# Left factors of a Strassen output projection formed in two portions, and gate rows and background sums issued under conditions

## Chip, cores and metric

The program runs on one NeuronCore of a Trainium2 chip. The metric is device time in microseconds (us), shown as the median of several runs; beside it stands one execution recorded by the hardware profiler, whose rows are used below. Engines: PE is TensorE, DVE is VectorE, ACT is ScalarE, POOL is GpSimd, SP issues the DMAs.

## What is computed

One hybrid streaming-encoder block on x of 1024 frames by 2048 channels, in float32:

```
mod = silu(c) @ w_ada + b_ada          # shift, scale, gate: 2048 each
h = rms(x) * norm_g * (1 + scale) + shift
a_q, a_k, a_v, a_z, g_q, g_f, g_i, g_z = split(h @ w_in)     # 8 groups of 1024 columns, 8 heads of 128
att = chunk_attention(a_q, a_k, a_v) * silu(a_z)   # each 64-frame chunk sees itself and 8 chunks before
hg  = hgrn2(g_q, g_f, g_i) * silu(g_z)             # gated linear recurrence, chunkwise
out = x + gate * (concat(att, hg) @ w_out)
```

## The kernel before

**Precision.** Every large product is made of three float32r matmuls: an operand is split into `hi`, a float32r copy written by ACT, and `lo`, the rest, written by DVE as a subtraction; the product is hi·hi + hi·lo + lo·hi. A matmul of 128 by 512 columns is the unit of TensorE's work.

**Input projection.** It runs head by head. A head has four slices of 192 matmuls: two slices `all` (q, k, v, i; each half of the frames), one `qf` (g_q and g_f, transposed) and one `zz` (both gate paths, transposed). The order is set by the list `slices` and the loop at L1037; the last head goes `qf`, `all`, `all`, `zz`. A slice fills four PSUM banks (`pj`), and at its end ACT and DVE evacuate them. Weights come in tiles `wraw`, fetched four steps ahead by SP and split two steps ahead (`ahead`, L982).

**Work in the background.** Attention (`att_mix`, L533), recurrence (`hg_mix`, L670) and the preparation of the output projection's right factors (`gate_gen`, L818, and then `wout_gen`, L853) are Python generators. The schedule is written out by hand: `run_ready` (L487) is called after each unit of matmuls, and lets every generator whose due time `st.t` has passed, by a model of the engines' times (`Engine`, costs at L45 to L61), issue its next piece. So the order of instructions on each engine is fixed when the program is built. A piece issued early waits on its engine, and what is behind it in that engine's queue waits too. `V.free` and `PE.free` are the model's times at which DVE and PE are done with what was issued; `wait(us)` puts a generator's due time that far behind PE's.

**Gate rows and right factors.** `gate_gen` sums the 2048 gate values in rows while heads 0 to 2 run. `wout_gen` then does, for each half q of the output columns: fetch the row sums `gl` from DRAM, split them (`ghi`, `glo`), sum them over the partitions on PE by a product with ones into the PSUM tile `gb`, and copy that to `gateb`. `gb` has the one buffer of the PSUM tag `ma`, which attention's score tile `att` uses too. Then, for each j of 0 to 7, it fetches two row blocks of w_out (`wor`), waits 20 us, multiplies both by the gate (DVE, 128x1024 each), forms five sums of quarter blocks (DVE, 128x512) and stores seven factors to `wdr`.

**Output projection.** Its seven products follow Strassen's scheme, in the order of `CHAIN` (L1001): m = 2, 3, 4, 5, 1, 6, 7, for q = 0 and then q = 1. A product has eight steps j, a step four units of three matmuls. Right factors come from `wdr`; the left factors of a pair j of blocks of the mixed activations are, with a11, a12, a21, a22 its four quarters: m = 1: a11 + a22; 2: a21 + a22; 3: a11; 4: a22; 5: a11 + a12; 6: a21 - a11; 7: a12 - a22. `out_sums` (L637) forms all five sums on DVE at once. For j = 0 to 6 the blocks were stored to `odr` and `reload_o` (L988) fetches them while the last slice runs: it is called at the end of each step kk of that slice (L1086), and the right and left factors of the first two steps are split there as well (L1088). For j = 7, the last head, `finish` (L648) calls `out_sums` as soon as both parts exist, which is after the last slice (its gate path is the last thing projected). `right_split` and `left_split` (L1011, L1020) make `whi`, `wlo` and `ahl` two steps ahead of PE.

Of the kernel before, what the change touches and what calls it, by code (L numbers as in the profile page):

```python
# [21 lines left out]
NK = D // 128  # L22
# [81 lines left out]
def tile_hymba(ctx, tc, x, c, norm_g, w_ada, b_ada, w_in, q_norm_g, k_norm_g, rel_bias,  # L104
# [428 lines left out]
    def att_mix(h, st, direct):  # L533
# [39 lines left out]
        for i in range(NT):  # L573
# [4 lines left out]
            n = i - j0 + 1  # L578
            w = n * 128
            p = MA("att")  # L580
            qs = slice(i * 128, (i + 1) * 128)
            m = sm.tile([128, 4], F32, tag="mstat", name="mstat", bufs=3)
# [35 lines left out]
            for j in range(n):  # L618
                PE.matmul(o, st["v"][:, j0 + j, :], PT[:, j * 128:(j + 1) * 128], start=(j == 0),
                          stop=(j == n - 1))  # L620
            A.activation(oT[:, qs], o, AF.Copy)
            yield
        done.add(("att", h))
# [13 lines left out]
    def out_sums(j, a11, a12, a21, a22):  # L637

        y, z = (hp.tile([128, 1024], F32, tag="h", name=n) for n in ("oay", "oaz"))
        a7 = half_tile(j)  # L640
        V.tensor_add(y[:, 512:1024], a21, a22)
        V.tensor_add(y[:, 0:512], a11, a22)
        V.tensor_add(z[:, 0:512], a11, a12)
        V.tensor_sub(z[:, 512:1024], a21, a11)
        V.tensor_sub(a7, a12, a22)
        OA[j] = {1: y[:, 0:512], 2: y[:, 512:1024], 3: a11, 4: a22, 5: z[:, 0:512], 6: z[:, 512:1024], 7: a7}

# [205 lines left out]
    def wout_gen():  # L853

        for q in range(2):
            a, hi, lo = T4("gl"), T4("ghi", dt=F32R), T4("glo", dt=F32R)
            DMA.dma_start(a, gdr[q])
            A.activation(hi, a, AF.Copy)
            V.tensor_sub(lo, a, hi.bitcast(F32))
            yield  # L860
            p = MA("gb")
            for s in (slice(0, 512), slice(512, 1024)):
                PE.matmul(p[:, s], onesr.to_broadcast([128, 128]), hi[:, s], start=True, stop=False)
                PE.matmul(p[:, s], onesr.to_broadcast([128, 128]), lo[:, s], start=False, stop=True)
            gate = T4("gateb")
            A.activation(gate, p, AF.Copy)
            gate = gate.rearrange("p (a b) -> p a b", a=2)
            yield
            for j in range(NH):
# [4 lines left out]
                yield  # L874
                V.tensor_mul(r1, r1, gate)
                yield
                V.tensor_mul(r2, r2, gate)
                yield
                b11, b12, b21, b22 = r1[:, 0, :], r1[:, 1, :], r2[:, 0, :], r2[:, 1, :]
                for ma, mb, fa, fb in ((1, 3, (V.tensor_add, b11, b22), (V.tensor_sub, b12, b22)),  # L880
                                       (4, 6, (V.tensor_sub, b21, b11), (V.tensor_add, b11, b12))):
                    o = T4("wos", (128, 2, 512))
                    fa[0](o[:, 0, :], *fa[1:])
                    yield
                    fb[0](o[:, 1, :], *fb[1:])
                    wait(2.0)
                    yield
                    DMA.dma_start(wdr[q, ma - 1, j], o[:, 0, :])
                    DMA.dma_start(wdr[q, mb - 1, j], o[:, 1, :])
                    if ma == 1:  # L890
                        DMA.dma_start(wdr[q, 1, j], b11)
                        DMA.dma_start(wdr[q, 4, j], b22)
                V.tensor_add(b21, b21, b22)
                wait(2.0)
                yield
                DMA.dma_start(wdr[q, 6, j], b21)

    def wait(us):
# [89 lines left out]
    def reload_o(j):  # L988

        oa, ob = (odr[slot[order[i]]] for i in (2 * j, 2 * j + 1))  # L990
        x_ = hp.tile([128, 1024], F32, tag="h", name="oax")
        r = T4("orl")
        DMA.dma_start(x_[:, 0:512], oa[:, 0:512])
# [43 lines left out]
    for sl in slices:  # L1037
        kind, h, half = sl
        sa, sh = st_att[h], st_hg[h]
        ps = [pj.tile([128, 512], F32, tag="pj", name="pj") for _ in range(4)]  # L1040
        if kind == "all":
            for k in range(NK):
                n = first[sl] + k
                w = W.get(n)
                for u in range(4):
                    ahead(n, u)
                    wide_unit(ps[u], hhi[k], hlo[k], 4 * half + u, w, k)
                    if k == NK - 1:
                        evac_all(sa, sh, ps[u], 4 * half + u)
                    run_ready()  # L1050
# [4 lines left out]
        else:  # L1055
            if sl == slices[0]:
                rest = MH("rest", (128, 256))
            for kk in range(8):
                n = first[sl] + kk * (2 if sl == slices[0] else 1)
                w = W.get(n)  # L1060
                last = kk == 7
                for u in range(4):
                    ahead(n, u)
                    b, hf = u // 2, u % 2
                    for i in range(2):
# [10 lines left out]
                if sl == slices[0]:  # L1076
# [6 lines left out]
                    if last:  # L1083
                        evac_vi(sa, sh, rest, 7)
                        done.update((("v", 0), ("v", NH)))
                if sl == slices[-1] and kk >= 1:  # L1086
                    reload_o(kk - 1)
                if sl == slices[-1] and kk >= 6:  # L1088
                    right_dma(2 * kk - 10)
                    right_split(kk - 6)  # L1090
                    left_split(kk - 6)
            if sl == ("zz", 0, 0):
# [51 lines left out]
    banks = [[pj.tile([128, 512], F32, tag="pj", name="pjo") for _ in range(4)], None]  # L1144
    n = 0
    for q in range(2):
        C = {}
        for m, s_, fresh in CHAIN:
# [4 lines left out]
            for j in range(NH):  # L1153
                for u in range(4):
# [13 lines left out]
                    PE.matmul(b, hl[:, 1, ts], whi, start=False, stop=last, skip_group_check=True)  # L1168
                    run_ready()
                    if last:  # L1170
                        if m == 2:
# [63 lines left out]
```

## Time and profile before

| what | us |
|---|---|
| median of 3 runs (2048.43 to 2049.7) | 2049.66 |
| the profiled execution's own time | 2050.44 |
| its span, first to last instruction | 2048.6 |
| PE busy in the span | 2005.3 |
| DVE busy | 1182.3 |
| ACT busy | 713.8 |

The span is what the profile's rows count in, from 0 to 2048.6; the execution's own time is 1.84 us longer. Busy PE time is not the same as PE at its peak: a row's duration includes the depth of the array, so the pace of matmuls is read from the distance of their starts. All instructions of the engines carry L87, the helper that records them; they are told apart by their tiles (`pj` input projection, `pjo` and `po` output projection, `gb` gate broadcast, `lv` and `Amat` the recurrence's levels). The input projection lasts to 1729.76, the output projection from there to the end.

### The profile page before, as it was taken

The numbers are of one execution on the slowest core, as the hardware profiler recorded it, in microseconds if no ns is written. First come the engines' busy times: TensorE is split into PE (matmuls) and PEld (weight loads), VectorE is DVE, ScalarE is ACT, GpSimd is POOL, SyncE is SP. The second block draws the span as 40 slices with busy tenths as digits, with TensorE's granted clock in tenths as the row PEclk, the third lists the DMA queues.
The fourth block names the chain that finished last, engine by engine and source line by source line (L and its number), as shares of the span: only waits on it lengthen the run. The fifth ranks groups of instructions, "written<-read, shape, count | busy, mean of one in ns | idle before, by whom it ended". The sixth has DMA issues, their size and how long they took to land.

```text
span 2048.6 us, 30420 instructions
## 1 busy us (share of the span) xinstructions
PE 2005.3 (98%) x11329; PEld 1654.9 (81%) x11329; DVE 1182.3 (58%) x2038; ACT 713.8 (35%) x1659; POOL 97.6 (5%) x104
## 2 busy tenths in 40 slices
PE   5999999999999999999999999999999999999999
PEld 4678878888888788888788888888888787888887
DVE  6885654466446545674467456533454547548547
ACT  6454323322332233223322332233221343454453
POOL 1540000000000000000000000000000000000000
PEclk9999999999999999999999999999999999999999
DMA  9982134324432453446445634132112234337336
GB/s 340 341 240 75 52 93 132 95 86 134 131 98 83 126 158 125 149 140 196 125 133 166 190 122 137 54 111 68 42 48 76 83 98 144 93 98 247 109 97 227
DMA packets 308234, 269.50 MB, mean 132 GB/s; under 512 B 20515, under 2 KB 250995, under 8 KB 308085
## 3 DMA queue, kind: packets, MB, share of 16 engines
q1 hardware_dynamic: 307828, 267.49, 42.8%
q8 instruction: 89, 1.46, 0.3%
q14 instruction: 61, 0.49, 0.1%
q0 software_dynamic: 256, 0.06, 0.0%
HBM read 221.32 MB, written 46.15 MB: 131 GB/s over the span
## 4 chain that ended last, share of the span: by engine, by line
PE 93%; DVE 3%; DMA 2%; ACT 1%; issue 1%; POOL 0%; SPq 0%; ACTq 0%; DVEq 0%; POOLq 0%
PE pj L87 62%; PE pjo L87 8%; PE po L87 6%; PE att L87 6%; PE pjn L87 2%; PE pjC L87 2%; PE lv L87 2%; PE hgo L87 1%; PE pjB L87 1%; DMA x<-in_x_dram 1%; PE qkT L87 1%; PE hgU L87 1%; PE xTp L87 1%; PE hgoT L87 0%; DVE Amat L87 0%
## 5 line engine op out<-in xcount | busy, mean ns | idle before, releaser
L87 DVE TENSOR_TENSOR wlo<-wraw,whi 128x512 fp32r<-128x512 f32 x488 | 336.2, 690 | 483.0 <-ACT whi L87 478.1
L87 ACT ACTIVATE whi<-wraw 128x512 fp32r<-128x512 f32 x488 | 307.3, 630 | 733.1 <-PE pj L87 500.9
L87 PE MATMUL pj<-hh,whi 128*128 128x512 f32 x1024 | 411.8, 402 | 0.4 <-ACT v L87 0.4
L87 PE MATMUL pj<-hl,whi 128*128 128x512 f32 x1024 | 400.0, 391 | 0.0
L87 PE MATMUL pj<-hh,wlo 128*128 128x512 f32 x1024 | 399.6, 390 | 0.0
L87 PE MATMUL pj<-whi,hh 128*128 128x512 f32 x896 | 357.9, 399 | 0.9 <-DVE z L87 0.5
L87 PE MATMUL pj<-whi,hl 128*128 128x512 f32 x896 | 350.3, 391 | 0.0
L87 PE MATMUL pj<-wlo,hh 128*128 128x512 f32 x896 | 349.7, 390 | 0.0
L87 PEld LDWEIGHTS pj<-hl,whi 128*128 128x128 f32 x1024 | 192.2, 188 | 41.6
L87 PEld LDWEIGHTS pj<-hh,whi 128*128 128x128 f32 x1024 | 192.5, 188 | 36.8 <-ACT v L87 0.8
L87 PEld LDWEIGHTS pj<-hh,wlo 128*128 128x128 f32 x1024 | 192.8, 188 | 34.3
L87 PEld LDWEIGHTS pj<-whi,hl 128*128 128x128 f32 x896 | 168.5, 188 | 36.2
L87 PEld LDWEIGHTS pj<-whi,hh 128*128 128x128 f32 x896 | 168.8, 188 | 35.3 <-DVE z L87 1.8
L87 PEld LDWEIGHTS pj<-wlo,hh 128*128 128x128 f32 x896 | 168.9, 188 | 31.6
L87 PE MATMUL pjo<-whi,ahl 128*128 128x512 f32 x512 | 161.2, 394 | 3.8 <-DVE ahl L87 3.7
L87 PE MATMUL po<-whi,ahl 128*128 128x512 f32 x384 | 119.2, 389 | 0.0
L87 PEld LDWEIGHTS pjo<-whi,ahl 128*128 128x128 f32 x512 | 97.3, 190 | 25.0 <-DVE ahl L87 4.5
L87 PE MATMUL pjo<-wlo,ahl 128*128 128x512 f32 x256 | 100.7, 393 | 2.1 <-DVE wlo L87 2.1
L87 ACT ACTIVATE P<-att,mstat 128x640 f32<-128x640 f32 (+2 forms) x64 | 42.4, 662 | 165.6 <-DVE mstat L87 165.6
L87 PEld LDWEIGHTS po<-whi,ahl 128*128 128x128 f32 x384 | 72.1, 188 | 15.0
L87 PE MATMUL po<-wlo,ahl 128*128 128x512 f32 x192 | 74.7, 389 | 0.0
L87 PEld LDWEIGHTS att<-PT,v 128*128 128x128 f32 x480 | 63.1, 191 | 5.6
(240 smaller groups left out, 2300.9 us busy)
## 6 DMA issues: line engine op xcount, KB each, us to landing
wraw<-in_w_in_dram SPq DMA_DIRECT2D x240, 192.0 KB, 3.1
wraw<-in_w_in_dram SPq DMA_DIRECT2D x272, 128.0 KB, 2.8
wada<-in_w_ada_dram SPq DMA_DIRECT2D x64, 512.0 KB, 8.1
wraw<-wdr SPq DMA_DIRECT2D x112, 256.0 KB, 2.7
wadag<-in_w_ada_dram SPq DMA_DIRECT2D x64, 256.0 KB, 2.8
wor<-in_w_out_dram SPq DMA_DIRECT2D x32, 512.0 KB, 5.5
wdr<-wos SPq DMA_DIRECT2D x64, 256.0 KB, 2.1
wraw<-in_w_in_dram SPq DMA_DIRECT2D x240, 64.0 KB, 2.9
```

The source lines that it names most:

```text
L87: return f(*a, **kw)
```

## The change

Five edits. `att_mix` and `wout_gen` mark in `done` when the one `ma` buffer holds a score tile or the gate broadcast, and each waits, before it asks for the buffer, until the other's mark is gone. `wout_gen` waits 8 us between the fetch of the row sums and their split, and 5 us between the split and the matmuls. `wout_gen`'s two gate multiplications become four of half the size, and each of its DVE instructions is issued only if the model has DVE free for 0.3 us and no slice is at its edge (the mark `edge`: the last two steps of an `all` slice, the last of another). `out_sums` forms only the sum of m = 2; the other four sums of each j are formed by `more_sums`, partly in place of a12 and a21, one after the second and one after the fourth unit of each step of the products m = 3 and m = 4 of q = 0. In the last slice `reload_o` and the first splits move from the end of a step to after its first unit is prepared (u = 1; u = 0 in the last step); the second reloaded tile comes from the pool `hp` and not from `big`.

```diff
--- before.py
+++ after.py
@@ -577,7 +577,11 @@
             j0 = max(0, i - 4)
             n = i - j0 + 1
             w = n * 128
+            while "gb" in done:
+                wait(0.3)
+                yield
             p = MA("att")
+            done.add("ma")
             qs = slice(i * 128, (i + 1) * 128)
             m = sm.tile([128, 4], F32, tag="mstat", name="mstat", bufs=3)
             Pt = sm.tile([128, 640], F32, tag="P", name="P")
@@ -619,6 +623,7 @@
                 PE.matmul(o, st["v"][:, j0 + j, :], PT[:, j * 128:(j + 1) * 128], start=(j == 0),
                           stop=(j == n - 1))
             A.activation(oT[:, qs], o, AF.Copy)
+            done.discard("ma")
             yield
         done.add(("att", h))
         yield from need(("z", h))
@@ -636,14 +641,18 @@
 
     def out_sums(j, a11, a12, a21, a22):
 
-        y, z = (hp.tile([128, 1024], F32, tag="h", name=n) for n in ("oay", "oaz"))
+        y = hp.tile([128, 1024], F32, tag="h", name="oay")
         a7 = half_tile(j)
         V.tensor_add(y[:, 512:1024], a21, a22)
-        V.tensor_add(y[:, 0:512], a11, a22)
-        V.tensor_add(z[:, 0:512], a11, a12)
-        V.tensor_sub(z[:, 512:1024], a21, a11)
-        V.tensor_sub(a7, a12, a22)
-        OA[j] = {1: y[:, 0:512], 2: y[:, 512:1024], 3: a11, 4: a22, 5: z[:, 0:512], 6: z[:, 512:1024], 7: a7}
+        OA[j] = {1: y[:, 0:512], 2: y[:, 512:1024], 3: a11, 4: a22, 5: a12, 6: a21, 7: a7}
+
+    def more_sums(j):
+
+        o = OA[j]
+        for f, m, a, b in ((V.tensor_add, 1, 3, 4), (V.tensor_sub, 7, 5, 4), (V.tensor_add, 5, 3, 5),
+                           (V.tensor_sub, 6, 6, 3)):
+            f(o[m], o[a], o[b])
+            yield
 
     def finish(kt, oT, direct):
 
@@ -855,15 +864,25 @@
         for q in range(2):
             a, hi, lo = T4("gl"), T4("ghi", dt=F32R), T4("glo", dt=F32R)
             DMA.dma_start(a, gdr[q])
+            wait(8.0)
+            yield
             A.activation(hi, a, AF.Copy)
             V.tensor_sub(lo, a, hi.bitcast(F32))
-            yield
+            wait(5.0)
+            yield
+            while "ma" in done:
+                wait(0.3)
+                yield
             p = MA("gb")
             for s in (slice(0, 512), slice(512, 1024)):
                 PE.matmul(p[:, s], onesr.to_broadcast([128, 128]), hi[:, s], start=True, stop=False)
                 PE.matmul(p[:, s], onesr.to_broadcast([128, 128]), lo[:, s], start=False, stop=True)
             gate = T4("gateb")
             A.activation(gate, p, AF.Copy)
+            done.add("gb")
+            wait(1.5)
+            yield
+            done.discard("gb")
             gate = gate.rearrange("p (a b) -> p a b", a=2)
             yield
             for j in range(NH):
@@ -872,16 +891,18 @@
                     DMA.dma_start(r.rearrange("p a b -> p (a b)"), wout_v[:, order[e], q * 1024:(q + 1) * 1024])
                 wait(OUTPACE)
                 yield
-                V.tensor_mul(r1, r1, gate)
-                yield
-                V.tensor_mul(r2, r2, gate)
-                yield
+                for r in (r1, r2):
+                    for i in range(2):
+                        yield from idle()
+                        V.tensor_mul(r[:, i, :], r[:, i, :], gate[:, i, :])
+                        yield
                 b11, b12, b21, b22 = r1[:, 0, :], r1[:, 1, :], r2[:, 0, :], r2[:, 1, :]
                 for ma, mb, fa, fb in ((1, 3, (V.tensor_add, b11, b22), (V.tensor_sub, b12, b22)),
                                        (4, 6, (V.tensor_sub, b21, b11), (V.tensor_add, b11, b12))):
                     o = T4("wos", (128, 2, 512))
+                    yield from idle()
                     fa[0](o[:, 0, :], *fa[1:])
-                    yield
+                    yield from idle()
                     fb[0](o[:, 1, :], *fb[1:])
                     wait(2.0)
                     yield
@@ -890,10 +911,17 @@
                     if ma == 1:
                         DMA.dma_start(wdr[q, 1, j], b11)
                         DMA.dma_start(wdr[q, 4, j], b22)
+                yield from idle()
                 V.tensor_add(b21, b21, b22)
                 wait(2.0)
                 yield
                 DMA.dma_start(wdr[q, 6, j], b21)
+
+    def idle():
+
+        while V.free > PE.free - 0.3 or "edge" in done:
+            wait(0.3)
+            yield
 
     def wait(us):
         Engine.cur.t = max(Engine.cur.t, PE.free) + us
@@ -988,8 +1016,7 @@
     def reload_o(j):
 
         oa, ob = (odr[slot[order[i]]] for i in (2 * j, 2 * j + 1))
-        x_ = hp.tile([128, 1024], F32, tag="h", name="oax")
-        r = T4("orl")
+        x_, r = (hp.tile([128, 1024], F32, tag="h", name=n) for n in ("oax", "oar"))
         DMA.dma_start(x_[:, 0:512], oa[:, 0:512])
         DMA.dma_start(x_[:, 512:1024], ob[:, 512:1024])
         DMA.dma_start(r[:, 0:512], ob[:, 0:512])
@@ -1036,12 +1063,15 @@
 
     for sl in slices:
         kind, h, half = sl
+        done.discard("edge")
         sa, sh = st_att[h], st_hg[h]
         ps = [pj.tile([128, 512], F32, tag="pj", name="pj") for _ in range(4)]
         if kind == "all":
             for k in range(NK):
                 n = first[sl] + k
                 w = W.get(n)
+                if k >= NK - 2:
+                    done.add("edge")
                 for u in range(4):
                     ahead(n, u)
                     wide_unit(ps[u], hhi[k], hlo[k], 4 * half + u, w, k)
@@ -1059,8 +1089,16 @@
                 n = first[sl] + kk * (2 if sl == slices[0] else 1)
                 w = W.get(n)
                 last = kk == 7
+                if last:
+                    done.add("edge")
                 for u in range(4):
                     ahead(n, u)
+                    if sl == slices[-1] and u == (kk < 7) and kk >= 1:
+                        reload_o(kk - 1)
+                        if kk >= 6:
+                            right_dma(2 * kk - 10)
+                            right_split(kk - 6)
+                            left_split(kk - 6)
                     b, hf = u // 2, u % 2
                     for i in range(2):
                         tr_unit(ps[u], 2 * kk + i, hf, w, i, slice(b * 128, (b + 1) * 128))
@@ -1083,12 +1121,6 @@
                     if last:
                         evac_vi(sa, sh, rest, 7)
                         done.update((("v", 0), ("v", NH)))
-                if sl == slices[-1] and kk >= 1:
-                    reload_o(kk - 1)
-                if sl == slices[-1] and kk >= 6:
-                    right_dma(2 * kk - 10)
-                    right_split(kk - 6)
-                    left_split(kk - 6)
             if sl == ("zz", 0, 0):
                 spawn(gate_gen())
             if kind == "qf":
@@ -1143,6 +1175,7 @@
     BLOCK = {"11": (1, 1), "12": (1, 2), "21": (2, 1), "22": (2, 2)}
     banks = [[pj.tile([128, 512], F32, tag="pj", name="pjo") for _ in range(4)], None]
     n = 0
+    sums = (None for j in range(NH) for _ in more_sums(j))
     for q in range(2):
         C = {}
         for m, s_, fresh in CHAIN:
@@ -1167,6 +1200,8 @@
                     PE.matmul(b, hl[:, 0, ts], wlo, start=False, stop=False, skip_group_check=True)
                     PE.matmul(b, hl[:, 1, ts], whi, start=False, stop=last, skip_group_check=True)
                     run_ready()
+                    if q == 0 and m in (3, 4) and u % 2:
+                        next(sums, None)
                     if last:
                         if m == 2:
                             if u == 0:
```

## Rows read from the trace of the kernel before

**Rows 1.** The page's chain of work that ended last, by engine.

```profile
PE 93%; DVE 3%; DMA 2%; ACT 1%; issue 1%; POOL 0%; SPq 0%; ACTq 0%; DVEq 0%; POOLq 0%
```

**Rows 2.** Waits of PE: who waited for whom, us in total, times, longest us.

```profile
PE pjo L87 <- DVE ahl L87: 3.7, 1, 3.7
...
PE gb L87 <- ACT ghi L87: 2.8, 2, 2.5
PE pjo L87 <- DVE wlo L87: 2.1, 1, 2.1
...
PE lv L87 <- DVE Amat L87: 1.6, 3, 0.7
...
PE gb L87 <- DVE glo L87: 1.4, 2, 0.8
```

**Rows 3.** Busy time by stretch: products m=2, m=3, m=1 of q=0; first gate broadcast.

```profile
core 0: us, PE busy (x) PEld busy (x) DVE busy (x) ACT busy (x) POOL busy (x), PEclk, DMA share, GB/s
1729.76:1761.16 31.40, 25.55 (x98) 20.04 (x97) 20.14 (x32) 12.14 (x22) 0.00 (x0) 0.89 0.24 69
1761.16:1782.92 21.76, 21.76 (x97) 18.02 (x97) 11.59 (x19) 9.89 (x18) 0.00 (x0) 1.00 0.35 96
...
1848.20:1869.96 21.76, 21.76 (x97) 18.02 (x97) 20.43 (x34) 9.23 (x16) 0.00 (x0) 1.00 0.72 237
703.61:714.15 10.54, 7.48 (x23) 5.48 (x22) 4.24 (x4) 2.65 (x4) 0.00 (x0) 0.68 0.51 181
```

**Rows 4.** Timeline of PE, 1729 to 1744: start, duration; in brackets idle time and releaser.

```profile
1734.95 0.50 PE L87 MATMUL pjo<-wlo,ahl 128*128 128x512 f32 x1 [2.08 <-DVE wlo L87]
...
1738.15 0.39 PE L87 MATMUL pjo<-wlo,ahl 128*128 128x512 f32 x1
1742.21 1.22 PE L87 MATMUL pjo<-whi,ahl 128*128 128x512 f32 x2 [3.68 <-DVE ahl L87]
```

**Rows 5.** Timeline of DVE, 1729 to 1742.

```profile
1730.59 0.69 DVE L87 SCALAR_TENSOR_TENSOR z<-z,pj 128x512 f32<-128x512 f32 x1 [0.68 <-ACT z L87]
1731.20 0.68 DVE L87 TENSOR_TENSOR oay<-orl,oax 128x512 f32<-128x512 f32 x1
...
1734.20 0.69 DVE L87 TENSOR_TENSOR wlo<-wraw,whi 128x512 fp32r<-128x512 f32 x1
...
1736.01 1.28 DVE L87 SCALAR_TENSOR_TENSOR oT<-hgoT,gcol,z 128x1024 f32<-128x1024 f32 x1
...
1738.46 1.29 DVE L87 TENSOR_TENSOR oay<-oT 128x512 f32<-128x512 f32 x2
...
1741.47 0.69 DVE L87 TENSOR_TENSOR ahl<-oay,ahl 128x512 fp32r<-128x512 f32 x1
```

**Rows 6.** Timeline of all engines around the first gate broadcast, 700 to 715.

```profile
701.26 0.38 SPq L857 DMA_DIRECT2D gl<-gdr  x1
...
704.06 0.39 PE L87 MATMUL pj<-whi,hl 128*128 128x512 f32 x1
...
705.80 1.06 ACT L87 ACTIVATE ghi<-gl 128x1024 fp32r<-128x1024 f32 x1 [4.76 <-DMA gl<-gdr]
...
709.62 1.91 PE L87 MATMUL hgoT<-ident,hgon 128*128 128x128 f32 x8
...
711.18 0.78 PE L87 MATMUL pj<-whi,hh 128*128 128x512 f32 x1
...
713.89 0.43 PE L87 MATMUL pj<-whi,hh 128*128 128x512 f32 x1
```

**Rows 7.** Timeline of all engines around the second gate broadcast, 998 to 1006.

```profile
998.58 0.39 PE L87 MATMUL pj<-whi,hl 128*128 128x512 f32 x1
...
1001.59 1.03 ACT L87 ACTIVATE gateb<-gb 128x1024 f32<-128x1024 f32 x1 [1.80 <-PE gb L87]
...
1004.72 0.50 PE L87 MATMUL pj<-hh,whi 128*128 128x512 f32 x1 [0.42 <-ACT v L87]
```

**Rows 8.** Instructions on `wor`: duration in ns min/median/max, first and last start.

```profile
L87 DVE TENSOR_TENSOR wos<-wor x64: 677/686/701, 737.3 to 1272.9; 128x512 f32<-128x512 f32 x64
...
L87 DVE TENSOR_TENSOR wor<-wor,gateb x32: 1217/1219/1226, 734.5 to 1263.7; 128x1024 f32<-128x1024 f32 x32
```

**Rows 9.** Timeline of DVE in the recurrence, ahead of a late `lv`.

```profile
877.95 2.36 DVE L87 TENSOR_TENSOR wor<-wor,gateb 128x1024 f32<-128x1024 f32 x2
```

**Rows 10.** DMA issues of the reload: count, KB each, median us to landing.

```profile
orl<-odr SPq DMA_DIRECT2D x14, 256.0 KB, 4.0
```

## Prediction

> **What bounds the kernel now.** I read the chain of waits first: PE holds 93% of it [rows 1], so time can only come from stretches in which PE stands still or is slow. The waits of PE come next [rows 2]; the waits that this change can reach are five: the output projection for `ahl` (3.7 us) and `wlo` (2.1), the gate broadcast for `ghi` (2.8) and `glo` (1.4), and the recurrence's levels for `Amat` (1.6). These idle times are only part of the price, so the table by stretch is read third [rows 3]. A product of the output projection is 96 matmuls and takes 21.76 us undisturbed, that is 0.227 us a matmul, 0.68 a unit, 2.72 a step. The first product, m = 2, has the same 96 and takes 31.40. Its granted clock is 0.89 on the mean, where the others have 1.00: after the wait of 3.68 us the two matmuls at 1742.21 take 1.22 us [rows 4], the pace of the 1.2 GHz level, and not that of 2.4. At half pace a lost share of 0.11 of 31.40 is about 3.4 us. The stretch around the first gate broadcast has 0.68, which is 0.32 of 10.54 or 3.4 us again [rows 3]. So a stall can cost nearly twice what the waits show.
>
> **Part 1, the seam between the projections.** What holds PE there is DVE's queue [rows 5]. The last gate evacuation `z` starts at 1730.59. Behind it stand, at a pitch of 0.60: five sums of the last reload (1731.20 to 1734.20), the splits `wlo` and `ahl` of step 1 and `wlo` of step 2 (to 1736.01), the two products `oT` of the last head (to 1738.46, so 2.45 us), its five sums, and at 1741.47 `ahl` of step 2, for which PE waits to 1742.21. The loss against an undisturbed product is 31.40 - 21.76 = 9.64.
> After the change the reload with its one sum and the splits of step 1 are issued at the start of the last step of the slice, a step's 24 matmuls or 5.4 us earlier, so ahead of all four `z`. Behind the last `z` remain `wlo` of step 2 (0.60), two `oT` (2.45), one sum (0.60): `ahl` of step 2 starts at 1731.20 + 3.65 = 1734.85 and PE can have it 0.74 later (the distance of 1741.47 and 1742.21), at 1735.59. PE needs it after two steps, at 1729.76 + 5.44 = 1735.20. I take a rest of 0.4 us and a **gain of 9.2**. Bounds: nothing left if the `oT` pieces are issued behind that split; if the three moved instructions stay behind `z` after all, 1.8 more, so 2.2 us of stall, and the lost clock of 3.4 again, a gain of only 4.0.
>
> **Part 2, the four postponed sums.** They add nothing in number: 32 sums of 0.60 pitch, 19.2 us, move from the last slice and the seam to the 16 steps of m = 3 and m = 4. There DVE has 11.59 busy of 21.76 in m = 3; 16 sums in a product raise that by 9.6 to 11 us, to 21 or 22 by durations, which overlap at their ends. By pitch a step holds two splits and two sums, 2.4 of 2.72 us; the last step of m = 3 adds four bank sums, 2.4 more, a backlog of 2.1 us that splits issued two steps (5.4 us) ahead can bear. The row that is nearest is m = 1, where DVE already carries 34 instructions and 20.43 us and the product still takes 21.76 [rows 3]. So I take 0; bounds are a gain of 0 and a loss of 19.2 with every sum exposed.
>
> **Part 3, the earlier reload.** Its sum can reach DVE before the data does: a landing takes 4.0 us [rows 10], and the call comes three units, about 4 us of matmuls, earlier. DVE could stand up to 4 us in each of seven steps. Queued behind it are the attention's scores of the last head and the next `wlo`, and that is prepared two steps ahead, each at least 5.4 us long here. I take 0; bounds 0 and 1 us. That cover is gone only in the last step, which is part 1's question.
>
> **Part 4, the gate broadcast.** Before, `gl` is fetched at 701.26, ACT waits for it until 705.80, and PE, after 704.06, until `ghi` and `glo` are there [rows 6]. From 704.06 to 713.89, when the pace is whole again, PE does 11 large matmuls (one, four of `gb`, six), 2.5 us at 0.227, and eight transposes, which took 1.56 at the low clock and so 0.8 at the whole one, with some 0.2 for the changes of shape: 3.5 of 9.83, a loss of 6.3. The second time 17 matmuls stand between 998.58 and 1004.72, 3.86 of 6.14, a loss of 2.3; it includes the late evacuation `v`, pushed back by the copy `gateb` (1.03 us) on ACT [rows 7]. With 8 us after the fetch (4.5 was needed) and 5 after the split (which takes ACT 1.06 and DVE about as long as a `wor` product, 1.22 [rows 8]) PE finds both. The copy `gateb` remains, at a place that I can't see; if it falls before an evacuation again it costs about the 0.42 us of [rows 7], each time; I take 0.6 for the two. **Gain 6.3 + 2.3 - 0.6 = 8.0**; bounds 4 and 8.6. The marks for the `ma` buffer hold attention back by a few us twice; behind it stand only its own later pieces, which end before the slice that uses them, so 0, at most 1.
>
> **Part 5, the conditions on DVE.** Two of the three waits for `Amat`, 1.4 us together, come after a pair of gate products of 2.36 us [rows 2, 9] with a split or a level's sums behind them. Four halves, each only where the model has DVE free, cost 64 times 0.60 in place of 32 times 1.13 (the pitch in the pair is 2.36 less the overlap), 2 us more of DVE work over hundreds of us, hidden behind matmuls. **Gain 1.4**; bounds 0 (the model, not the chip, says when DVE is free) and 2. The work is stretched: it now goes from 734.5 to 1276 [rows 8], 16 units of about 35 us, 20 of them the fixed wait. The output projection wants the first factors near 1713, so from a start near 718 a unit may take 62 us; I expect about 45.
>
> **The sum.** 9.2 + 8.0 + 1.4 = 18.6; I take 0.5 off for small waits at new places. 2050.44 - 18.1 = 2032.3 for an execution like the profiled one; the median of the runs is 0.78 lower, so 2031.6.
>
> **Rivals.** *The seam is only half mended* (DVE's order behind `z` stays): part 1 gives 4.0 instead of 9.2, 2036.8. For it: PE's order and DVE's depend on due times that I can't read off; against it: the moved splits wait on nothing that the last step makes. *The gate broadcast still stalls PE*, because SP reaches the fetch late: it would cost part 4 whole, 2039.6. Against it: SP issued `gl` ahead of PE's need in both rows. *The clock falls at a smaller stall.* Here 2.08 us of idle left the pace whole (the matmuls from 1734.95 to 1738.15 are about 0.23 apart), and 3.68 did not [rows 4]. Should the 0.4 us left at the seam be enough together with other idle time, 3.4 us come back: 2035.0. The Trainium skill ("TensorE: Matmul & The Clock Gate", Part 1: The HAM clock gate) has the low level as the default that activity lifts, judged in windows that run free of the program; by that the same stall may be caught in one run and not in the next. *Slower:* the left factors are late in m = 3 and m = 4. The place is DVE behind the sums; the point is when a step's DVE work with its waits for ACT's halves passes 2.72 us, against 2.4 now; with all 19.2 us exposed and one fall of the clock the price is 22.6, and 2031.6 + 22.6 = 2054.2. Against it stands m = 1 in [rows 3]. *The change does nothing*: pieces come out in the same order by the model, and what the seam gains is given back; 2049 to 2050.
>
> **How the numbers follow.** A measurement of this kernel can tell about 0.2%, 4.1 us, from no change. Chances: forecast 0.74, half-mended seam 0.09, gate stall 0.04, clock 0.03, all of them faster by more than that: 0.90. No change 0.04. Slower 0.06. The lowest end is every term whole, 9.6 + 8.6 + 2 = 20.2, or 2029.5, with half a us for its spread, 2029. The upper end takes in the gate rival, 2040; beyond it lies 1 in 10, below 2029 less than that.
>
> **What would show it.** The stretch of m = 2 takes 22 us, at a granted clock of 1.00; the waits of PE no longer list `gb`, and `ahl` and `wlo` with under 1 us; m = 3 and m = 4 hold about 35 DVE instructions each and still take 21.76; the last `wor` row lies between 1350 and 1550. A product m = 3 or m = 4 of over 22 us, a new stretch of low clock, or `wor` rows beyond 1700 would prove me wrong.

## The result and the profile after

| what | before | after |
|---|---|---|
| median of 6 runs, us | 2049.78 (2048.43 to 2051.2) | 2035.99 (2034.46 to 2040.83) |
| profiled execution's own time | 2050.44 | 2038.13 |
| its span | 2048.6 | 2036.3 |

The ratio of after to before is 0.9936, with a 95% interval of 0.9923 to 0.9949: 13.8 us faster in the median, where 18.1 were forecast; the time lies within the range that was forecast, 2029 to 2040.

The waits of PE in the changed kernel, in the columns of [rows 2]:

```profile
PE hgoT L87 <- DVE hgon L87: 2.7, 2, 1.5
PE att L87 <- DVE P L87: 2.2, 2, 1.9
...
PE pj L87 <- DVE z L87: 1.5, 3, 0.5
PE lv L87 <- DVE Amat L87: 1.5, 2, 1.3
```

The waits for `ghi`, `glo`, `ahl` and `wlo` are gone from the list. The wait for `Amat` is not: it is one of 1.3 us and one of 0.2 now, where [rows 2] has three of up to 0.7. A wait of 1.9 us for `P`, the attention's probabilities, is new, and so is a second one for `hgon`, the recurrence's scaled output; the waits for `z`, the gate evacuation, grew to three. Busy time by stretch, in the columns of [rows 3] (the last slice; m = 2, 3 and 4 of q = 0):

```profile
1662.68:1726.93 64.25, 61.16 (x338) 52.60 (x336) 28.08 (x54) 22.79 (x67) 3.65 (x2) 1.00 0.47 152
1726.93:1748.75 21.82, 21.82 (x98) 17.94 (x96) 13.36 (x21) 10.95 (x20) 0.00 (x0) 1.00 0.29 86
1748.75:1770.51 21.76, 21.76 (x98) 18.02 (x96) 19.85 (x33) 10.05 (x18) 0.00 (x0) 1.00 0.34 97
1770.51:1792.27 21.76, 21.76 (x98) 18.02 (x96) 21.19 (x37) 10.47 (x19) 0.00 (x0) 1.00 0.35 98
```

The product m = 2 takes 21.82 us at a granted clock of 1.00, against 31.40 at 0.89 [rows 3]. VectorE carries 33 and 37 instructions in m = 3 and m = 4, and both take 21.76. But the last slice takes 64.25. Before, it took 61.00, with more work on VectorE (40.18 us, 75 instructions, against 28.08 and 54):

```profile
1668.76:1729.76 61.00, 61.00 (x337) 52.67 (x336) 40.18 (x75) 21.62 (x65) 3.27 (x2) 1.00 0.47 156
```

So 3.25 us were lost where VectorE had been relieved. Its timeline in the last slice of the changed kernel shows how:

```profile
1679.61 0.69 DVE L87 TENSOR_TENSOR oay<-oar,oax 128x512 f32<-128x512 f32 x1 [2.72 <-DMA oar<-odr]
1680.39 0.11 DVE L87 MEMSET att<- 64x64 f32 x1
...
1681.01 0.82 DVE L87 TENSOR_REDUCE mstat<-att 128x1 f32<-128x640 f32 x1
...
1683.04 0.55 DVE L87 TENSOR_SCALAR P<-P,mstat 128x640 f32<-128x640 f32 x1
```

and PE's in the same stretch:

```profile
1683.74 0.74 PE L87 MATMUL att<-ident,P 128*128 128x128 f32 x5 [1.87 <-DVE P L87]
...
1688.20 1.09 PE L87 MATMUL hgoT<-ident,hgon 128*128 128x128 f32 x8 [1.22 <-DVE hgon L87]
```

The one sum of the first reload, `oay`, stands at the head of VectorE's queue for 2.72 us until its data has landed. Attention's scores are behind it, and PE waits for the probabilities that come of them. In the kernel before, the same reload's first sum started without idle time, behind attention's work:

```profile
1686.58 0.55 DVE L87 TENSOR_SCALAR P<-P,mstat 128x640 f32<-128x640 f32 x1
1687.05 0.68 DVE L87 TENSOR_TENSOR oay<-orl,oax 128x512 f32<-128x512 f32 x1
```

**Where the time went.** By distances of matmul starts, the whole execution divides into six stretches; the last two, which the table leaves out, are nearly alike in every run (282.7 from the end of m = 2 to the last matmul, and 4.9 behind it, 5.7 in three runs). Each row is one profiled execution.

| us | start to first matmul of head 0's last two slices | from there to the last slice | last slice | m = 2 |
|---|---|---|---|---|
| before | 160.68 | 1508.08 | 61.00 | 31.23 |
| after | 161.25 | 1501.44 | 64.25 | 21.82 |
| after, once more | 165.08 | 1500.88 | 64.29 | 21.83 |
| reloads at the end of a step | 161.57 | 1501.21 | 60.79 | 21.83 |
| reload DMAs early, sums at the end | 159.86 | 1501.02 | 60.79 | 21.84 |
| reloads and first splits at the end | 159.98 | 1501.16 | 60.80 | 23.63 |
| all sums at once | 165.48 | 1501.47 | 66.85 | 24.37 |
| no waits at the gate rows | 160.84 | 1507.56 | 64.09 | 21.84 |
| no condition on VectorE | 159.69 | 1500.82 | 63.99 | 21.84 |
| a mark for the levels | 161.96 | 1500.95 | 63.92 | 21.84 |
| only the first reload at the end | 160.32 | 1504.07 | 61.29 | 21.82 |
| states wait for the edge | 159.33 | 1502.39 | 60.80 | 21.85 |
| DMAs early, no condition | 159.87 | 1503.89 | 60.75 | 21.82 |

From before to after, the sum of the differences is 0.57 - 6.64 + 3.25 - 9.41 = -12.2; the two spans differ by 12.3. The first column, where none of the edits lies, spreads by 6 us between executions, which can move the median of a few runs by 1 or 2 us. The other three columns are steady to some tenths where no edit reaches them, but for a fall of the clock that added 2 to 2.5 us to the second column in two runs (last section); the experiments are read by them.

### The profile page after: what moved, and what is told of

Its sections match the earlier page's. It is cut to its first block, busy times and chain, and to the rows that moved or that the text cites. A ratio compares the mean times of both kernels' runs of the same rounds, so it can differ in the third digit from the quotient of the medians.

```text
span 2036.3 us, 30467 instructions
## 1 busy us (share of the span) xinstructions
PE 1998.5 (98%) x11329; PEld 1650.8 (81%) x11329; DVE 1185.5 (58%) x2070; ACT 713.7 (35%) x1659; POOL 99.0 (5%) x104
## 4 chain that ended last, share of the span: by engine, by line
PE 92%; DVE 2%; DMA 2%; issue 2%; SPq 1%; ACT 1%; POOL 0%; POOLq 0%; DVEq 0%; ACTq 0%
PE pj L87 61%; PE pjo L87 8%; PE po L87 6%; PE att L87 6%; PE pjn L87 2%; PE pjC L87 2%; PE lv L87 2%; PE hgo L87 1%; PE pjB L87 1%; DMA wraw<-in_w_in_dram 1%; DMA x<-in_x_dram 1%; PE qkT L87 1%; PE hgU L87 1%; SPq L201 1%; DVE hgS L87 0%
```

## Experiments

All edits are to the changed kernel; ratios are to the kernel before on the same chip. The experiments ran on three chips, on which the kernel before took 2049.3, 2051.0 and 2050.5 us, so across them the ratios compare, and not the times.

**The changed kernel once more.**

> The changed kernel once more, beside the next three on the same chip. My theory of what kept it short of the forecast (reload theory): in the last slice the one sum of the first reload stands at the head of VectorE's queue until its data has landed (2.72 us in the profile), attention and recurrence of the last head queue behind it, and PE waits about 3.4 us; how long depends on the landing, so the median moves with it: 2034.5 to 2037. A rival (drift theory): the missing 4 us are many small waits spread over the heads, and the last slice takes 61 us here.

2037.45 us, ratio 0.9944 (0.9932 to 0.9957). The last slice has 64.29 us again: the loss there is not a chance of one execution, and the 61 of the drift theory did not come. The median is 0.45 above the range that I gave. The profiled execution of this run took 2041.51, 3.4 more than the first one; its first column alone is 3.8 longer.

**The reloads back at the end of a step.**

```diff
-                    if sl == slices[-1] and u == (kk < 7) and kk >= 1:
+                    if sl == slices[-1] and u == 0 and kk == 7:
                         reload_o(kk - 1)
...
+                if sl == slices[-1] and 1 <= kk < 7:
+                    reload_o(kk - 1)
...
```

> The changed kernel with the reloads of steps 1 to 6 of the last slice back at the end of their step (the last step's stays early). Reload theory: no instruction of VectorE waits for a reload, the last slice takes 61 us where the changed kernel's profile has 64.2, the seam keeps its 21.8 us, and the time falls by 1.5 to 3.4 us to about 2033. Drift theory: the same time as the changed kernel, within 0.5 us.

2034.39 us, 0.9924 (0.9910 to 0.9937). The last slice is at 60.79, and m = 2 stays at 21.83:

```profile
1662.79:1723.58 60.79, 60.79 (x338) 52.59 (x337) 27.82 (x54) 22.67 (x67) 3.27 (x2) 1.00 0.49 161
```

The reload theory's 61 us came out, and the median is 3.1 us below the changed kernel's on the same chip; the drift theory wanted no change.

**The DMAs early, the sums at the end.**

```diff
-        out_sums(j, x_[:, 0:512], r[:, 0:512], r[:, 512:1024], x_[:, 512:1024])
+        return lambda: out_sums(j, x_[:, 0:512], r[:, 0:512], r[:, 512:1024], x_[:, 512:1024])
...
+                        held = reload_o(kk - 1)
...
+                if sl == slices[-1] and 1 <= kk < 7:
+                    held()
...
```

> As the run before, but the reload's four DMAs keep their early place and only the sum moves to the end of the step. Reload theory (the sum's place in VectorE's queue is what costs): as fast as with both at the end, about 2033, with no wait of VectorE for a reload. Rival (the DMAs' place costs, through SP's queue or by crowding the weights): the 64 us of the last slice stay and so does 2036.

2032.70 us, 0.9918 (0.9905 to 0.9932), the lowest time of all runs, 16.6 us below before and faster than the changed kernel (2037.45 on the same chip); by its ratio one other run is level with it (0.9916, below). The slice is at 60.79 again, so the place of the DMAs costs nothing; it is the place of the sum in VectorE's queue. The timeline of VectorE there has the sum behind attention's work and without idle time:

```profile
1676.06 0.11 DVE L87 MEMSET att<- 64x64 f32 x1 [0.96 <-PE att L87]
...
1678.70 0.55 DVE L87 TENSOR_SCALAR P<-P,mstat 128x640 f32<-128x640 f32 x1
1679.17 0.68 DVE L87 TENSOR_TENSOR oay<-oar,oax 128x512 f32<-128x512 f32 x1
```

Between the profiled executions of this run and the one before it, 1.9 us apart, 1.7 lie in the first column of the table (159.86 against 161.57), where the edit has no part. That the 1.7 us between the medians come from there too is likely, but the other executions have no trace to show it.

**Reloads and first splits at the end.**

```diff
-                    if sl == slices[-1] and u == (kk < 7) and kk >= 1:
-                        reload_o(kk - 1)
-                        ...
+                if sl == slices[-1] and kk >= 1:
+                    reload_o(kk - 1)
+                if sl == slices[-1] and kk >= 6:
+                    ...
```

> All reloads and the splits of the first two steps of the output projection back at the end of their step, as before the change; the sums stay in two portions. Seam theory of the forecast: one sum and two splits, 1.8 us of VectorE, stand behind the last gate evacuation again, the split of step 2 comes about 1.5 to 2.2 us too late, m = 2 takes 23.3 to 24.0 us at whole clock (or up to 27.4 if the clock falls), while the last slice has 61 us: 2034 to 2036. Rival (the early place is needless, the split sums alone mend the seam): m = 2 takes 21.8 us, and 2033.

2036.44 us, 0.9939 (0.9927 to 0.9951), 0.44 above the range that I gave. m = 2 takes 23.63 us, as expected, and its timeline of VectorE has the three instructions behind the last `z` again:

```profile
1722.77 0.69 DVE L87 SCALAR_TENSOR_TENSOR z<-z,pj 128x512 f32<-128x512 f32 x1 [0.67 <-ACT z L87]
1723.37 0.68 DVE L87 TENSOR_TENSOR oay<-oar,oax 128x512 f32<-128x512 f32 x1
1723.97 0.69 DVE L87 TENSOR_TENSOR wlo<-wraw,whi 128x512 fp32r<-128x512 f32 x1
1724.57 0.69 DVE L87 TENSOR_TENSOR ahl<-oay,ahl 128x512 fp32r<-128x512 f32 x1
```

So the early place in the last step is worth 1.8 us. The clock stayed at the 2.4 GHz level here, a granted clock of 1.00:

```profile
1721.94:1745.57 23.63, 22.37 (x97) 17.86 (x96) 15.16 (x24) 11.98 (x22) 0.00 (x0) 1.00 0.32 89
```

**All sums at once.**

```diff
         OA[j] = {...}
+        for _ in more_sums(j):
+            pass
...
-                    if q == 0 and m in (3, 4) and u % 2:
-                        next(sums, None)
```

> The changed kernel, but all five sums of a pair formed at once where the first one is (early place kept); the steps of m = 3 and m = 4 get none. Theory of the forecast (the seam was VectorE's queue): four sums, 2.4 us, more between the last gate evacuation and the split of step 2, which came just in time in the changed kernel, so m = 2 takes 24.0 to 25 us, or up to 28 if the clock falls; in the last slice another 28 sums make the wait behind the first reload no shorter, 64 us or more. 2039 to 2044. Rival (the early place alone mends the seam): m = 2 stays at 21.8 us and the time within 1 us of the changed kernel's 2036 to 2037.

2041.20 us, 0.9954 (0.9942 to 0.9967). m = 2 takes 24.37, with one wait for `ahl`:

```profile
1742.16 0.73 PE L87 MATMUL pjo<-whi,ahl 128*128 128x512 f32 x2 [2.31 <-DVE ahl L87]
```

The last slice takes 66.85, with a wait for `P` of 2.9 us and the low clock behind it (a granted clock of 0.95 over the slice):

```profile
1666.95:1733.80 66.85, 63.97 (x337) 55.07 (x336) 45.20 (x82) 22.69 (x67) 3.27 (x2) 0.95 0.45 146
```

The profiled execution of this run, 2048.34, is the slowest of its seven; 4.2 of what it has over the first profile of the changed kernel lie in the first column, so only the other columns are read here. Without the postponed sums 2.5 us of the seam's stall come back, without the early place 1.8; neither of the two edits alone removes it.

**No waits at the gate rows.**

```diff
-            wait(8.0)
-            yield
             A.activation(hi, a, AF.Copy)
             V.tensor_sub(lo, a, hi.bitcast(F32))
-            wait(5.0)
             yield
```

> The changed kernel without the waits of 8 and 5 us around the split of the row sums; the marks for the shared buffer stay. Theory of the forecast: PE waits again for the row sums' landing, about 2.5 us and 0.6 us at the first gate broadcast with a fall of the clock (6.3 us in all), and 1 to 2 us at the second, so 4 to 8.5 us more than the changed kernel: 2040 to 2045. Rival (the marks alone do it, or the new place hides the landing): within 1 us of the changed kernel.

2045.18 us, 0.9981 (0.9969 to 0.9993), just above what I expected; three of its ten executions took 2050 to 2052, the profiled one 2043.71. PE waits as before the change, and the clock falls once (0.98 from 695 to 800):

```profile
695.00:800.00 105.00, 101.69 (x465) 83.78 (x464) 50.69 (x86) 40.53 (x114) 3.27 (x2) 0.98 0.49 153
```

```profile
707.47 0.50 PE L87 MATMUL gb<-ghi,onesr 128*128 128x512 f32 x1 [2.55 <-ACT ghi L87]
...
708.73 0.66 PE L87 MATMUL gb<-glo,onesr 128*128 128x512 f32 x1 [0.76 <-DVE glo L87]
```

The second column goes from 1501.4 to 1507.6: the two waits are worth 6.1 us together, and the marks for the shared buffer, which stay in this run, do not give it. What each wait is worth by itself was not tried.

**No condition on VectorE's work.**

```diff
-        while V.free > PE.free - 0.3 or "edge" in done:
-            wait(0.3)
-            yield
+        yield from ()
```

> The changed kernel with the condition of the right factors' VectorE work taken out (no wait for a free VectorE, none for the edges of slices; the halves stay). Forecast: 1.4 us more, in waits of PE for the recurrence's levels. My theory now: the condition does nothing there, since the model prices the recurrence's small matmuls far over what they take and so believes VectorE free when it is not; the two waits of 0.7 to 0.9 us come back in place of the one of 1.3, and the time is within 1 us of the changed kernel's 2036 to 2037; the right factors are done near 1300 us instead of 1417.

2038.08 us, 0.9940 (0.9921 to 0.9960), with 1500.82 in the second column against 1501.44: the condition gains nothing that shows. The last `wor` sum starts at 1312.8, against 1416.3 with it. I expected two waits for `Amat` of 0.7 to 0.9 us back in place of the one of 1.3. That is not what came: the longest is 0.3, and one of 0.8 for `hgK`, one of the levels' operands, is new:

```profile
PE lv L87 <- DVE hgK L87: 0.8, 1, 0.8
...
PE lv L87 <- DVE Amat L87: 0.7, 3, 0.3
```

So the condition, put in against the waits for `Amat`, had moved work in such a way that one of them was longer: a wait of 1.2 to 1.3 us stands at the same place in eight of the nine profiles taken with the condition as it is (the ninth is the run without the waits at the gate rows), and in neither of the two without it. VectorE's timeline in the changed kernel shows that the condition does not do what it is written for:

```profile
871.66 1.80 DVE L87 COPY_PREDICATED Amat<-masks,lv 32x256 f32<-32x256 uint8 x4
873.49 2.50 DVE L87 TENSOR_TENSOR wor<-wor,gateb 128x512 f32<-128x512 f32 x4
876.02 1.29 DVE L87 TENSOR_TENSOR wos<-wor 128x512 f32<-128x512 f32 x2
877.24 0.68 DVE L87 TENSOR_TENSOR hgQ<-hgQ,hgR 128x512 f32<-128x512 f32 x1
```

Six instructions, 3.75 us, stand in one row between the recurrence's copy and its next products, where [rows 9] had a pair of 2.36. PE then waits before the next level:

```profile
880.62 1.15 PE L87 MATMUL lv<-hgQ,hgK 128*64 128x64 f32 x32 [1.29 <-DVE Amat L87]
```

Why the condition let them through is argued, not shown: the kernel's model takes at least 0.108 us for each of the 32 small matmuls of a level, 3.5 us, and the trace has 0.76 for a level (two records each):

```profile
873.60 0.76 PE L87 MATMUL lv<-hgQ,hgK 128*32 128x32 f32 x64
```

so in the model PE's time runs ahead, and VectorE seems to have had nothing to do.

**A mark for the levels.**

```diff
+        done.add("lev")
         p = MH("lv", (128, 8, 128))
         level(p, 32)
...
+        done.discard("lev")
         dec = lev
...
-        while V.free > PE.free - 0.3 or "edge" in done:
+        while V.free > PE.free - 0.3 or "edge" in done or "lev" in done:
```

> The changed kernel with one more condition: the right factors' VectorE work also waits while a head's recurrence goes through its levels. My theory (the model's price of the levels' small matmuls opens the condition wrongly): no gate product stands between two copies into Amat any more, the wait of PE for Amat falls from 1.3 us to the 0.4 or less of heads without this work, gain about 1 us. Rival (the levels wait for VectorE's own recurrence work): the wait of 1.3 us stays and so does the time.

2036.84 us, 0.9929 (0.9914 to 0.9944). Its waits of PE:

```profile
PE hgo L87 <- DVE hgS L87: 1.3, 2, 0.7
...
PE lv L87 <- DVE Amat L87: 0.2, 1, 0.2
```

The wait for `Amat` fell from 1.5 to 0.2, as I expected, and 1.3 us for the recurrence's states, `hgS`, took its place: the second column is 1500.95, 0.5 less, where I expected 1. So it was the background work between the levels that held `Amat` up. That the model's price let this work in is not shown by this run, since the mark keeps it out whatever the model says.

**Only the first reload at the end.**

```diff
-                    if sl == slices[-1] and u == (kk < 7) and kk >= 1:
+                    if sl == slices[-1] and kk >= 2 and u == (kk < 7):
...
+                if sl == slices[-1] and kk == 1:
+                    reload_o(kk - 1)
```

> The changed kernel with only the first of the seven reloads back at the end of its step; the other six stay early. Reload theory in its narrow form (only the first reload is late, since the six others have their data before VectorE gets to them): the last slice takes 60.8 us, no wait of VectorE for a reload. Rival (each early sum delays the last head a little, or the next reload takes the first one's place): 62 us or more.

2034.13 us, 0.9916 (0.9901 to 0.9931). The last slice takes 61.29: nearly all of the loss was the first reload's, but the next one takes its place in part:

```profile
1685.77 0.69 DVE L87 TENSOR_TENSOR oay<-oar,oax 128x512 f32<-128x512 f32 x1 [1.71 <-DMA oar<-odr]
```

So the narrow form of the theory was too narrow, and the rival's 62 us or more did not come either. The second column, 1504.07, has the fall of the clock that the last section shows.

**The states wait for the edge** (with the edit of the third experiment).

```diff
...
+        while "edge" in done:
+            wait(0.3)
+            yield
         S = T4("hgS", (128, 8, 128))
...
```

> Reload DMAs early and their sums at the end of the step, and the recurrence's chain of states (hgS, 2.3 us of VectorE) also waits for the edge of a slice to pass. The profile of the changed kernel has three waits of PE for the gate evacuation z, each 0.67 us with its change of pace, where that chain stands ahead of z. If it is the chain's place that costs, these three go and the input projection from the first head to the last slice takes about 1499 us instead of 1501, so about 2031 us in all. Rival (the states are then late for the recurrence's output): the waits move to hgo, and the time stays at 2032.7.

2035.41 us, 0.9926 (0.9913 to 0.9939). No wait for `z` is left, but the second column is 1502.39, not 1499. Its waits of PE:

```profile
PE lv L87 <- DVE Amat L87: 2.3, 3, 1.2
...
PE hgo L87 <- DVE hgS L87: 1.5, 7, 0.3
```

So the waits went elsewhere: seven for the states themselves, as the rival had it, 1.5 us in all, and one more for `Amat`. The rival was right in kind; the second column is 1.4 worse than in the third experiment, where the rival had no change. How the later states bring the wait for `Amat` was not followed further.

**DMAs early, no condition.** The edits of the third and the seventh experiment together.

> Reload DMAs early, sums at the end of the step, and the condition on the right factors' VectorE work taken out again. If the condition is worth nothing (run without it above: 1500.8 us from the first head to the last slice, against 1501.4), 2032 to 2033, the same as with it, with m = 2 at 21.8 and the last slice at 60.8 us. Rival (the condition is worth the 1.4 us of the forecast): about 1.4 us more.

2035.23 us, 0.9922 (0.9909 to 0.9936). The time is 2 us above the 2032 to 2033 that I expected, on another chip; the ratio is level with the third experiment's 0.9918. m = 2 and the last slice are as expected. The second column has 1503.89, some 2.5 us of which lie in one slice near 300 us, ahead of everything that the edits touch (a fall of the clock, below). Without that it is 1501.4, within some tenths of the 1501.0 with the condition; the 1.4 us of the rival are not there.

## Why the prediction was right, and where it was off

**The seam (part 1): right.** 9.2 us were forecast and 9.41 came (31.23 - 21.82; by starts m = 2 took 31.23 before, the row in [rows 3] reaches 0.17 further). The order on VectorE was the one that I worked out: `z`, the split of step 2, the two `oT`, one sum, and then `ahl` of step 2, which starts 0.61 behind its sum in the changed kernel:

```profile
1727.76 0.69 DVE L87 SCALAR_TENSOR_TENSOR z<-z,pj 128x512 f32<-128x512 f32 x1 [0.67 <-ACT z L87]
...
1732.02 0.69 DVE L87 TENSOR_TENSOR ahl<-oay,ahl 128x512 fp32r<-128x512 f32 x1
```

It is there by 1732.76, by the 0.74 us of the prediction. Step 2 of PE starts at 1726.93 + 5.44 = 1732.37, so by my working a rest of 0.4 us should have been left. PE lists no wait, since I had put the need too early: the split is read by the third matmul of the step, not by the first:

```profile
1732.60 0.39 PE L87 MATMUL pjo<-wlo,ahl 128*128 128x512 f32 x1
1732.82 0.67 PE L87 MATMUL pjo<-whi,ahl 128*128 128x512 f32 x2
```

So the seam is mended with almost nothing to spare. The rival of a half-mended seam is what the fourth experiment builds: 23.63 us without the early place. It lost 1.8 us, where I had priced 5.2: the 1.8 us of moved work came, the 3.4 of a low clock did not, behind a wait of 1.23 us.

**The postponed sums (part 2): right.** m = 3 and m = 4 stayed at 21.76 each, with VectorE busy for 21.19 us in m = 4. The slower rival had its place here and did not come.

**The earlier reload (part 3): wrong.** This is the step that failed. I saw that the sum could reach VectorE ahead of its data and wrote that it could stand there up to 4 us; I took 0, with 1 us as the upper end, because `wlo` is prepared two steps ahead. That covers `wlo` alone. I named the attention's scores as queued behind the sum and gave no cover for them, and the recurrence's `hgon` I did not name; PE waited for both, 1.87 and 1.22 us. The term measured 3.25 us (64.25 - 61.00), and the second and third experiments give 3.5 back. VectorE stood for one reload only, the first, and its data took longer than the 4.0 us that I read, which count from the issue of one DMA: SP issued the four DMAs of this reload one behind the other,

```profile
1673.26 0.34 SPq L1020 DMA_DIRECT2D oax<-odr  x1
...
1675.52 0.42 SPq L1023 DMA_DIRECT2D oar<-odr  x1
```

and the sum started 6.35 us behind the first of them.

**The gate rows (part 4): right in kind and near in size.** In slices, 102.34 - 96.08 = 6.3 us were gained at the first broadcast, as forecast; these rows, before and after, hold it:

```profile
694.36:796.70 102.34, 99.28 (x450) 81.25 (x448) 48.66 (x80) 36.66 (x98) 3.27 (x2) 0.97 0.56 169
```

```profile
695.04:791.12 96.08, 95.95 (x450) 79.30 (x448) 43.97 (x75) 36.49 (x98) 3.64 (x2) 1.00 0.50 150
```

At the second one the two slices around its old place gained 101.10 - 99.17 = 1.9, against 2.3; a new wait of 0.5 us for `z` is in that:

```profile
903.62:1004.72 101.10, 99.56 (x477) 82.32 (x475) 55.21 (x91) 36.21 (x96) 3.27 (x2) 1.00 0.61 186
```

```profile
898.62:997.79 99.17, 98.61 (x473) 81.57 (x472) 49.83 (x89) 34.72 (x96) 3.27 (x2) 1.00 0.52 156
```

The copy `gateb`, for which I took 0.6 off, cost nothing that the waits show. The rival that SP reaches the fetch late did not occur the first time: `ghi` started at 710.70, without idle time, for a fetch issued at 701.95. The second time it did occur, and was absorbed: SP issued the fetch, behind a store of a right factor, only at 1067.85, and ACT stood idle for it:

```profile
1071.82 1.06 ACT L87 ACTIVATE ghi<-gl 128x1024 fp32r<-128x1024 f32 x1 [1.92 <-DMA gl<-gdr]
```

ACT came to the split about 2 us behind the fetch there, and not 8; PE came to the broadcast at 1079.5 and lists no wait for it.

**The condition on VectorE (part 5): wrong.** Of the 1.4 us nothing came: the wait for `Amat` is 1.5 us in all, where it was 1.6. The term came out at the lower bound that I named, that the model and not the chip says when VectorE is free; six instructions went through where VectorE was needed, and without the condition this wait is not there at all. The stretching of the work was forecast right, to 1416 of an expected 1350 to 1550. The second column's gain of 6.64 is the 8.2 of part 4 less a remainder of 1.6 us in the other slices, where I had allowed 0.5 for small waits at new places.

In sum: 9.41 + 6.64 - 3.25 - 0.57 of the start = 12.2 for the profiled execution, where 18.1 were forecast. 3.25 of the missing 5.9 are part 3, 1.4 part 5, 0.6 the start, 1.1 the waits at new places; parts 1 and 4 gave 0.4 more than forecast.

That the time stayed in the range is in part luck. Its upper end, 2040, was set for the gate rival, which did not come; part 3 alone went 2.25 us past its own upper end of 1 us, and part 5 came to the bottom of its bounds.

## What to carry to other kernels

An instruction that uses fetched data should be put into an in-order queue not when its fetch is issued but when its data can be there; issuing the fetch early was free here (60.79 us in the last slice with the DMAs early or late), and the use early stopped everything behind it. When such a use is moved, list all the work queued behind it and ask of each piece, not of the most frequent one, how far ahead of its reader it runs. And before a stall is priced, look at the granted clock behind it: by the granted clock, both large stalls of the kernel before cost about 3.4 us more than their idle time.

## What the runs showed of the hardware

Whether a wait of PE is followed by the 1.2 GHz level does not follow from the length of the wait alone. In head 0's recurrence, in work that only one edit moves, PE waits for `hgon` in all profiled executions but the one with that edit; 1.16 to 1.77 us in ten of them, all without a fall, and in the other two 2.00 and 2.35 us with one. The wait of 2.00, and the granted clock around it:

```profile
297.84 1.45 PE L87 MATMUL hgoT<-ident,hgon 128*128 128x128 f32 x8 [2.00 <-DVE hgon L87]
```

```profile
290.00:305.00 15.00, 13.00 (x55) 10.53 (x54) 7.41 (x11) 2.90 (x8) 2.07 (x1) 0.89 0.59 178
```

These are the runs with only the first reload at the end, and with the DMAs early and no condition; both have 2 to 2.5 us more in the slice that holds the wait. At that one place the longer waits are the ones with a fall. But at the seam 2.31 us (all sums at once) and 2.08 [rows 4] brought no fall. Waits of 2.88 (all sums at once, last slice), of 2.46 with 0.60 behind it and of 3.68 did. The Trainium skill ("TensorE: Matmul & The Clock Gate", Part 1: The HAM clock gate) says that the windows in which activity is judged run free of the program; waits of nearly one length with and without a fall agree with that, and no run here tells more.

The start, too, differs between executions of one kernel: up to 160 us the granted clock was 0.99 in the first profile of the changed kernel and 0.96 in the second, whose first column is 3.8 us longer:

```profile
0.00:160.00 160.00, 135.75 (x892) 98.89 (x893) 124.34 (x253) 89.98 (x179) 57.69 (x80) 0.99 0.96 298
```

```profile
0.00:160.00 160.00, 137.02 (x874) 100.55 (x875) 122.13 (x249) 89.04 (x175) 57.63 (x80) 0.96 0.94 296
```

What decides it was not tried.
